# A conditioning projection moved from TensorE matmuls to products summed by VectorE

## The chip, the cores and the metric

The kernel runs as one program on one core of one Trainium2 chip. The metric is the device time of one execution in microseconds (us); lower is better. Inputs are in HBM, in layouts that the host has packed, and everything is float32.

## The reference, cut to what matters

The program is two blocks of a network over 256 tokens of width 1024. The first block is a gated delta rule and a dilated attention side by side (the "mixers"), merged through two gates, and a feed-forward part that gathers expert rows. The second block is conditioned: each of its four sublayers uses a shift, a scale and a gate computed from one vector `c`:

```python
cond = jax.nn.silu(c)                                        # c: (1, 1024)
for layer in range(DEPTH_2):                                 # two layers
    mod = jnp.einsum('bd,sde->sbe', cond, ada_w[layer]) + ada_b[layer][:, None, :]
    ...
    shift, scale, gate = jnp.split(mod[0], 3, axis=-1)
    h = rms_norm(x, norm_g[layer, 0]) * (1.0 + scale[:, None, :]) + shift[:, None, :]
```

`ada_w` has 2 x 2 x 1024 x 3072 values, 48 MB. The result `mod` is 4 x 3072 numbers, held in the kernel as a tile of 128 partitions x 96 columns: column o holds outputs 128 o to 128 o + 127. It depends on `c` and the weights alone, so it can be computed at any time before the second block.

## The kernel before, in words

The kernel is written with a tile framework. The code names the engine of each instruction; a planner, which works with its own cost estimates, then fixes the order on each engine and on each DMA queue, and on the chip every engine runs its list in that order. The planner takes what is ready and prefers what stands earlier in the program; work far down in the program runs early if its inputs are there.

The conditioning runs beside the mixers (`mixers`, L442 on). It is a Python generator, `gen4 = ada_pe(am, 0, 96, NQ[0])` (L452), that the mixers' code advances by `quad()`: two steps before the first norm, one after each of six convolution pairs (L465 on, the quad after L490), one after each of 20 doubling steps of the triangular inverses (L624 to L640), one after each of four steps of the state scan, six in the projections of the second pair of attention heads, one in each of eight softmax blocks. What is left runs in a burst just before the merge (`for _ in gen4`, after L791).

One step of `ada_pe` (L415 to L419) loads a tile of 128 x 4 x 512 weights (1 MB, two buffers) by SyncE's queue and multiplies it by one column of silu(c): four matmuls, each with a single column as its stationary operand, that write rows 0, 32, 64 and 96 of one PSUM bank. Eight steps sum up 2048 outputs as four rows. After eight steps the rows are copied to SBUF by four ScalarE copies of 1 x 512 (L424) into a buffer that GpSimd has cleared (L422), turned to columns by four TensorE transposes (L426), and copied to `mod` by VectorE (L427). There are 48 weight steps and six such ends.

The mixers' own work is a stream of projections. A 512 KB weight tile (`load`, L131, four buffers) is split into a high part by ScalarE (L141) and a low part by VectorE (L142), two buffers each, and TensorE multiplies both against the normed input: 24 matmuls of 128 x 256 for each tile (L159, L160, L162; L265, L266, L270 where tokens are on the output's partitions). Beside them run the convolutions on VectorE (L485, L487), the inverses (TensorE L627, L632, L637; ScalarE L629; VectorE's predicated copies L633 and L638), the scan (L672 to L690) and the attention softmax (L726 to L748). PSUM is eight banks of 2 KB: four for tag `pa`, three for tag `pb`, one for the conditioning's sums (`psx`).

After the merge the branch projection (L805) and the output projection follow; in the latter `ada_done` (L431) adds the bias to `mod`, transposes it and writes it to HBM.

Of the kernel before, what the change touches and what calls it, by code (L numbers as in the profile page):

```python
# [9 lines left out]
F32 = mybir.dt.float32  # L10
# [4 lines left out]
AF = mybir.ActivationFunctionType  # L15
ALU = mybir.AluOpType
AX = mybir.AxisListType
PSUM = bass.MemoryType.PSUM
DRAM = bass.MemoryType.DRAM

P = 128
T = 256
D = 1024
KC = 8
EPS = 1e-6
NEG = -1e30
CAP = 64
NADA = 24
NQ = (2, 2)
NG = 11  # L30


# [16 lines left out]
def body(tc, A, out, stop=None, start=None):  # L49
    nc = tc.nc  # L50
    pe, dve, act, pool, sp = nc.tensor, nc.vector, nc.scalar, nc.gpsimd, nc.sync
# [6 lines left out]
    def pa(shape, name="pa"):  # L58
        return psa.tile(shape, F32, name=name, tag="pa")

    PB = {}

    def open_pb(n):
        PB["es"] = ExitStack()
        PB["b"] = PB["es"].enter_context(tc.tile_pool(name="psb", bufs=n, space=PSUM))
        PB["x"] = PB["es"].enter_context(tc.tile_pool(name="psx", bufs=4 - n, space=PSUM)) if n < 4 else None

    def pb(shape, name="pb"):
        return PB["b"].tile(shape, F32, name=name, tag="pb")
# [7 lines left out]
    x = open_x()  # L77
# [24 lines left out]
    def col(name, i=0, n=None):  # L102
        o = COLS[name][0] + i
        return cols[:, o:o + (1 if n is None else n)]

    ident, iota = C("ident"), C("iota")
    half = [cf[:, NCONST - 2 + i:NCONST - 1 + i] for i in range(2)]
    ones_r = cst.tile([P, P], F32R, name="ones_r")
# [25 lines left out]
    def split(w, n=1024, lo=None, of=None):  # L134
        if of and type(of[0]) is not type(w):
            wh, wl = [of[0].tile([P, n], F32R, name=of[1] + i, tag=of[1], bufs=2) for i in "hl"]
        elif of:
            wh, wl = of
        else:
            wh, wl = [ST["p"].tile([P, 1024], F32R, name="w" + i, tag="w" + i, bufs=ST["sp"]) for i in "hl"]  # L140
        act.copy(wh[:, :n], w[:, :n])  # L141
        (lo or dve).tensor_sub(wl[:, :n], w[:, :n], wh[:, :n].bitcast(F32))  # L142
        return wh, wl
# [94 lines left out]
    def norm_t(pool_, src, a_cols, b_cols, xh, xl, ready=None, copy=None):  # L238

        ss = sums(pool_, 4, "nss") if ready is None else ready  # L240
        xt = [pool_.tile([P, 4, T], F32, name="nxt", tag=f"nxt{i}", bufs=1) for i in range(2)]
        for n in range(4):
            chunk_t(pool_, src, n, ss if ready is None else None, xt[n // 2][:, n % 2 * 2:n % 2 * 2 + 2],
                    copy)
        rs = rstd(pool_, ss, "nr")
        norm_scale([xt[k // 4][:, k % 4] for k in range(KC)], rs, a_cols, b_cols, xh, xl)
        return rs
# [110 lines left out]
    mod = cst.tile([P, 96], F32, name="mod")  # L358
    mod_d = drm.tile([4, 3 * D], F32, name="mod_d")

    def ada(pool_, o0, o1, nw, hl_tag, eng, after=None):

        cs = pool_.tile([P, 8], F32, name="cs", tag="cs", bufs=1)
        act.activation(cs, col("c", 0, 8), AF.Tanh, scale=0.5)
        dve.tensor_scalar(cs, cs, 0.5, 0.5, op0=ALU.mult, op1=ALU.add)
        dve.tensor_mul(cs, cs, col("c", 0, 8))
        pend = []

        def column_sums(acc):
            hl = split(acc, 512, pool, (pool_, hl_tag))  # L370
            ps = pa([P, 512], "ps_ada")
            for i in range(2):
                pe.matmul(ps, ones_r, hl[i][:, 0:512], start=i == 0, stop=i == 1)
            return ps

        def to_columns(o, ps):
            for j in range(4):
                js = slice(j * P, (j + 1) * P)
                dve.tensor_tensor_reduce(ps[:, js], ps[:, js], ident, 1.0, 0.0, ALU.mult, ALU.add, mod[:, o + j:o + j + 1])

        for o in range(o0, o1, 4):
            acc = pool_.tile([P, 512], F32, name="aacc", tag="aacc", bufs=1)
            for k in range(KC):
                w = pool_.tile([P, 512], F32, name="aw", tag="aw", bufs=nw)
                if after is not None and 2 * (o - o0) + k < nw:
                    pool.tensor_copy(w[:, 0:1], after)
                sp.dma_start(w, A["ada_w"][o * 2 + k])
                if k == 0:
                    eng.tensor_scalar_mul(acc, w, cs[:, 0:1])
                elif eng is pool:  # L390
                    pool.tensor_scalar_mul(w, w, cs[:, k:k + 1])
                    pool.tensor_add(acc, acc, w)
                else:
                    dve.scalar_tensor_tensor(acc, w, cs[:, k:k + 1], acc, op0=ALU.mult, op1=ALU.add)
                if k == 4 and pend:
                    to_columns(*pend.pop())
                if k < KC - 1:
                    yield
            pend.append((o, column_sums(acc)))
            yield  # L400
        if pend:
            to_columns(*pend.pop())

    def ada_pe(pool_, o0, o1, nw):


        cs = pool_.tile([P, 8], F32, name="cs", tag="cs", bufs=1)
        act.activation(cs, col("c", 0, 8), AF.Tanh, scale=0.5)
        dve.tensor_scalar(cs, cs, 0.5, 0.5, op0=ALU.mult, op1=ALU.add)
        dve.tensor_mul(cs, cs, col("c", 0, 8))  # L410
        for o in range(o0, o1, 16):
            n = min(4, (o1 - o) // 4)
            ps = PB["x"].tile([P, 512], F32, name="ps_ada", tag="px")
            for k in range(KC):
                w = pool_.tile([P, 4, 512], F32, name="awp", tag="awp", bufs=nw)  # L415
                sp.dma_start(w, A["ada_w"].rearrange("(s j k) p n -> s k p j n", j=4, k=KC)[o // 16, k])
                for j in range(n):
                    pe.matmul(ps[32 * j:32 * j + 1], cs[:, k:k + 1], w[:, j], start=k == 0, stop=k == KC - 1)
                yield  # L419
            pc = pa([P, 4, P], "pc_ada")  # L420
            r = pool_.tile([P, 4, 512], F32, name="arow", tag="awp", bufs=nw)[:, 0]
            pool.memset(r, 0.0)  # L422
            for j in range(n):
                act.copy(r[32 * j:32 * j + 1], ps[32 * j:32 * j + 1])  # L424
            for c in range(4):
                pe.transpose(pc[:, c], r[:, c * P:(c + 1) * P], ident)  # L426
            dve.tensor_copy(mod[:, o:o + 4 * n].rearrange("p (j c) -> p j c", c=4),  # L427
                            pc[:, :, 0:32 * n:32].rearrange("p c j -> p j c"))
            yield

    def ada_done(pool_):  # L431
# [9 lines left out]

    def mixers():  # L442
        es = ExitStack()
        open_pb(3)
        mx = es.enter_context(tc.tile_pool(name="mx", bufs=1))
        am = es.enter_context(tc.tile_pool(name="am", bufs=1))

        def quad(n=1):
            for _ in range(n):
                next(gen4, None)  # L450

        gen4 = ada_pe(am, 0, 96, NQ[0])  # L452
        cx[0] = mx.tile([P, 4 * P], F32, name="cx")
        def tl(shape, name, tag=None, bufs=1, dt=F32, p_=None):
            return (p_ or mx).tile(shape, dt, name=name, tag=tag or name, bufs=bufs)
# [1 line left out]
        with tc.tile_pool(name="nrm", bufs=1) as np_:  # L457
            xh, xl = None, None
            xh = mx.tile([P, KC, T], F32R, name="xh", tag="xh")
            xl = mx.tile([P, KC, T], F32R, name="xl", tag="xl")  # L460
            ws = [load(A["w_in"][i]) for i in range(2)]
            quad(NQ[1])
            norm_t(np_, x, col("norm_mix", 0, 8), None, xh, xl)

        oah = mx.tile([P, 4, T], F32R, name="oah")  # L465
        oal = mx.tile([P, 4, T], F32R, name="oal")
# [6 lines left out]
        with tc.tile_pool(name="cv", bufs=1) as cv:  # L473
            for c in range(0, 12, 2):
# [3 lines left out]
                ps = pa([P, 2, T])  # L478
                proj_pair(ps, A["w_in"][c:c + 2] if c else [lambda: ws[0], lambda: ws[1]], xh, xl, (pool, pool) if c == 0 else (None, None), c == 0)
                act.copy(cin[:, :, 2:T + 2], ps)  # L480
                acc = cv.tile([P, 2, T], F32, name="cacc", tag="cacc", bufs=2)
                th = cv.tile([P, 2, T], F32, name="cth", tag="cth", bufs=2)
                for j in range(2):
                    w = lambda i: col("conv", (c + j) * 4 + i)
                    dve.tensor_scalar_mul(acc[:, j], cin[:, j, 0:T], w(0))  # L485
                    for i in range(1, 4):
                        dve.scalar_tensor_tensor(acc[:, j], cin[:, j, i:i + T], w(i), acc[:, j],  # L487
                                                 op0=ALU.mult, op1=ALU.add)
# [8 lines left out]
                if c == 0:  # L497
                    ab = tl([P, 2, 16], "ab")
                    ps = proj_small(dq, A["w_ab"], 16, xh, xl, "ab")
# [20 lines left out]
                if c == 4:  # L520
                    ps = pa([P, 80])
# [25 lines left out]
            r = stat_rsqrt(cv, pst.rearrange("p a b -> p (a b)"), 8, 1.0, 4 * EPS, "l2")  # L547
            for c in range(0, 8, 2):
                ps = pa([P, 2, T])
                for j in range(2):  # L550
                    stat_bc(ps[:, j], r, c + j)
                dve.scalar_tensor_tensor(qkv[:, c:c + 2], qkv[:, c:c + 2], (P ** -0.5) if c < 4 else 1.0, ps,
                                         op0=ALU.mult, op1=ALU.mult)
# [4 lines left out]
        for b in range(2):  # L558
            for o, base in ((kt, 4), (vt, 8)):
                ps = pa([P, 4, P])  # L560
# [254 lines left out]
                ada_done(am)  # L815
        es.close()
        PB["es"].close()
        open_pb(4)

# [1086 lines left out]
        if stop == "mix":  # L1908
            return finish()
    if start == "peer":  # L1910
        open_pb(4)
        with tc.tile_pool(name="adp", bufs=1) as adp:
            for _ in ada(adp, 0, NADA, 2, "gc", dve):
                pass
# [5 lines left out]
            ST["es"].close()  # L1920
            return finish()
    if start not in (None, "peer"):
        open_pb(4)
        with tc.tile_pool(name="adp", bufs=1) as adp:
            for _ in ada(adp, 0, 96, 2, "gc", dve):
                pass
            ada_done(adp)
# [101 lines left out]
def _pack(I):  # L2029
    v = {}  # L2030
# [64 lines left out]
        mw[:, :, 2 * n:2 * n + 2] = I[nm].reshape(2, 16, 2, 4, P, 512).transpose(0, 1, 2, 4, 3, 5).reshape(2, 16, 2, P, 2048)  # L2095
    mw[:, :, 4:6] = I["moe_w2_2"].reshape(2, 16, 4, P, 2, 512).transpose(0, 1, 4, 3, 2, 5).reshape(2, 16, 2, P, 2048)
    v["moe_w"] = mw
    v["ada_w"] = I["ada_w_2"].reshape(4, 8, P, 6, 512).transpose(0, 3, 1, 2, 4).reshape(192, P, 512)
    return v


# [24 lines left out]
```

## Time and profile before

| | us |
|---|---|
| median of 3 runs | 2070.19 (2065.85 to 2072.55) |
| the profiled execution | 2081.53 |
| its span | 2079.7 |

| engine | busy us | share of the span | instructions |
|---|---|---|---|
| TensorE matmul (PE) | 1833.2 | 88% | 9963 |
| TensorE weight load (PEld) | 1191.3 | 57% | 9963 |
| VectorE (DVE) | 1075.7 | 52% | 2616 |
| ScalarE (ACT) | 603.9 | 29% | 1232 |
| GpSimd (POOL) | 449.4 | 22% | 407 |

The span is the time from the first to the last instruction of the profiled execution. Matmuls are pipelined and the profile models their ends, so a busy TensorE is not TensorE at its peak. The granted clock is the share of full speed that TensorE was given. A float32 matmul is recorded as two instructions. Names such as `awp<-in_ada_w` say what is written from what.

### The profile page before, as it was taken

The numbers are of one execution on the slowest core, as the hardware profiler recorded it, in microseconds if no ns is written. First come the engines' busy times: TensorE is split into PE (matmuls) and PEld (weight loads), VectorE is DVE, ScalarE is ACT, GpSimd is POOL, SyncE is SP. The second block draws the span as 40 slices with busy tenths as digits, with TensorE's granted clock in tenths as the row PEclk, the third lists the DMA queues.
The fourth block names the chain that finished last, engine by engine and source line by source line (L and its number), as shares of the span: only waits on it lengthen the run. The fifth ranks groups of instructions, "written<-read, shape, count | busy, mean of one in ns | idle before, by whom it ended". The sixth has DMA issues, their size and how long they took to land. (4 is left out here: it accounts for less than half of the span.)

```text
span 2079.7 us, 27097 instructions
## 1 busy us (share of the span) xinstructions
PE 1833.2 (88%) x9963; PEld 1191.3 (57%) x9963; DVE 1075.7 (52%) x2616; ACT 603.9 (29%) x1232; POOL 449.4 (22%) x407
## 2 busy tenths in 40 slices
PE   7999999989787787877887789988999899979998
PEld 6787897779743332333333369774444599854443
DVE  6545452346857577577575554763222369642222
ACT  4433342335321111121111143642111364421110
POOL 2100000001454444444444311010000154310000
PEclk8999998999989999999999999898999999989999
DMA  9666643755699999999999957136999483469995
GB/s 320 200 228 192 213 150 100 275 168 167 239 426 427 427 427 426 427 410 427 427 421 427 427 179 268 52 136 285 419 419 419 174 292 119 179 243 419 419 420 226
DMA packets 122679, 624.82 MB, mean 300 GB/s; under 512 B 11535, under 2 KB 16495, under 8 KB 65035
## 3 DMA queue, kind: packets, MB, share of 16 engines
q1 hardware_dynamic: 85675, 354.54, 45.8%
q0 software_dynamic: 36864, 268.45, 30.7%
q8 instruction: 83, 1.36, 0.3%
q14 instruction: 57, 0.46, 0.1%
HBM read 621.80 MB, written 1.16 MB: 300 GB/s over the span
## 5 line engine op out<-in xcount | busy, mean ns | idle before, releaser
L986 PE MATMUL acc<-uv,dg 128*128 128x512 f32 x1024 | 498.6, 645 | 123.7 <-ACT dg L984 123.6
L986 PEld LDWEIGHTS acc<-uv,dg 128*128 128x128 f32 x1024 | 205.9, 206 | 414.4 <-issue 242.3
L974 DVE CUSTOM_DVE_ANT_0 uv<-uv,xn 128x1024 f32<-128x1024 f32 x256 | 316.9, 1242 | 205.7 <-DMA uv<-in_puv,ix 198.9
L973 POOL DMA_INDIRECT uv<-in_puv,ix x256 | 287.5, 1123 | 339.6 <-PE acc L986 236.0
L142 DVE TENSOR_TENSOR wl<-w,wh 128x1024 fp32r<-128x1024 f32 x129 | 160.6, 1249 | 166.8 <-ACT wh L141 109.4
L141 ACT CAST wh<-w 128x1024 fp32r<-128x1024 f32 x166 | 173.6, 1049 | 247.7 <-PE pb L160 71.9
L1631 PE MATMUL ph<-mw,xg 128*64 128x512 f32 x1024 | 226.0, 600 | 6.8 <-DVEq L1557 6.8
L1631 PEld LDWEIGHTS ph<-mw,xg 128*64 128x64 f32 x1024 | 76.1, 138 | 153.3 <-issue 152.2
L142 POOL TENSOR_TENSOR wl<-w,wh 128x1024 fp32r<-128x1024 f32 x37 | 89.0, 2408 | 244.3 <-PE pa L270 158.6
L980 ACT ACTIVATE ac<-ac 128x4 f32<-128x4 f32 (+1 forms) x65 | 13.4, 206 | 430.1 <-DVE ac L974 430.1
L159 PE MATMUL pa<-xh,wh 128*128 128x256 f32 x480 | 121.5, 290 | 2.1 <-ACT wh L141 2.1
L160 PE MATMUL pa<-xl,wh 128*128 128x256 f32 x480 | 119.5, 286 | 0.0
L1667 PE MATMUL pa<-mw,hT 128*64 128x512 f32 x512 | 116.9, 595 | 0.0
L1639 DVE TENSOR_TENSOR h<-h,ph 128x256 f32<-128x256 f32 x32 | 12.0, 418 | 200.5 <-PE ph L1631 200.5
L159 PEld LDWEIGHTS pa<-xh,wh 128*128 128x128 f32 x480 | 93.3, 194 | 6.5 <-ACT wh L141 3.6
L160 PEld LDWEIGHTS pa<-xl,wh 128*128 128x128 f32 x480 | 93.2, 194 | 0.0
L984 ACT ACTIVATE dg<-cf,ac 128x128 f32<-128x128 f32 x256 | 82.5, 392 | 22.1 <-DVE ac L981 20.5
L159 PE MATMUL pb<-xh,wh 128*128 128x256 f32 x352 | 88.4, 287 | 0.0
L160 PE MATMUL pb<-xl,wh 128*128 128x256 f32 x352 | 88.2, 286 | 0.0
L162 PE MATMUL pa<-xh,wl 128*128 128x256 f32 x480 | 69.7, 290 | 19.7 <-POOL wl L142 15.8
L162 PEld LDWEIGHTS pa<-xh,wl 128*128 128x128 f32 x480 | 62.9, 195 | 22.1 <-POOL wl L142 16.6
L1667 PEld LDWEIGHTS pa<-mw,hT 128*64 128x64 f32 x512 | 36.7, 137 | 67.1 <-issue 66.2
(617 smaller groups left out, 2991.7 us busy)
## 6 DMA issues: line engine op xcount, KB each, us to landing
mw<-in_moe_w SPq DMA_DIRECT2D x192, 1024.0 KB, 16.6
awp<-in_ada_w SPq DMA_DIRECT2D x48, 1024.0 KB, 5.6
w<-in_w_in SPq DMA_DIRECT2D x68, 512.0 KB, 5.0
w<-in_hg_c SPq DMA_DIRECT2D x22, 512.0 KB, 4.0
w<-in_wq SPq DMA_DIRECT2D x16, 512.0 KB, 3.6
w<-in_nsa_c SPq DMA_DIRECT2D x16, 512.0 KB, 8.3
w<-in_w_br SPq DMA_DIRECT2D x8, 512.0 KB, 4.3
w<-in_w_out SPq DMA_DIRECT2D x8, 512.0 KB, 3.5
```

Of the source, the lines that this page charges most:

```text
L141: act.copy(wh[:, :n], w[:, :n])
L142: (lo or dve).tensor_sub(wl[:, :n], w[:, :n], wh[:, :n].bitcast(F32))
L159: pe.matmul(ps, wh[:, k], xh[:, k], start=k == 0, stop=False)
L160: pe.matmul(ps, wh[:, k], xl[:, k], start=False, stop=False)
L162: pe.matmul(ps, wl[:, k], xh[:, k], start=False, stop=k == nk - 1)
L973: pool.indirect_dma_start(w, None, A["puv"], bass.IndirectOffsetOnAxis(ap=ix[b][:, k:k + 1], axis=0))
L974: dve.tensor_tensor_reduce(w[:, 0:D], w[:, 0:D], xn[:, b], 1.0, 0.0, ALU.mult, ALU.add, h[:, s:s + 1])
L980: act.activation(hs, hs, AF.Gelu_apprx_tanh)
L984: act.mul(dg, ident, hs[:, i:i + 1])
L986: pe.matmul(acc[b][n], dg, w[:, D + 512 * n:D + 512 * n + 512], start=k == 0, stop=k == P - 1)
L1631: pe.matmul(ps[64 * i:64 * i + 64], xg[:, k, CAP * i:CAP * i + CAP], r3(w[4 * c + 2 * (k // 4) + i], 4)[:, k % 4], start=k == 0, stop=k == ...
L1667: pe.matmul(ps[64 * i:64 * i + 64], hT[:, f, 64 * i:64 * i + 64], w2[n][i][:, f], start=f == 0, stop=f == 3)
```

## The change

`ada` and `ada_pe` are replaced by one generator on VectorE. The host packs `ada_w` as 96 tiles of 128 output columns (partitions) x 1024 inputs, 512 KB each. The row silu(c) is brought to all partitions once (`cr`, a broadcast load of 512 KB, then ScalarE and VectorE on 128 x 1024). One step loads one tile (three buffers of 4 KB for each partition) and runs one `tensor_tensor_reduce`: it multiplies the tile by `cr` in place and writes the sum over the 1024 inputs to one column of `mod`. There are no matmuls, no PSUM bank and no end of a group. `quad` advances two steps; the first quad stands behind the norm instead of ahead of it; tag `pb` gets the fourth PSUM bank.

```diff
-    def open_pb(n):
+    def open_pb():
         PB["es"] = ExitStack()
-        PB["b"] = PB["es"].enter_context(tc.tile_pool(name="psb", bufs=n, space=PSUM))
-        PB["x"] = PB["es"].enter_context(tc.tile_pool(name="psx", bufs=4 - n, space=PSUM)) if n < 4 else None
+        PB["b"] = PB["es"].enter_context(tc.tile_pool(name="psb", bufs=4, space=PSUM))
...
-        for o in range(o0, o1, 16):
-            n = min(4, (o1 - o) // 4)
-            ps = PB["x"].tile([P, 512], F32, name="ps_ada", tag="px")
-            for k in range(KC):
-                w = pool_.tile([P, 4, 512], F32, name="awp", tag="awp", bufs=nw)
-                sp.dma_start(w, A["ada_w"].rearrange("(s j k) p n -> s k p j n", j=4, k=KC)[o // 16, k])
-                for j in range(n):
-                    pe.matmul(ps[32 * j:32 * j + 1], cs[:, k:k + 1], w[:, j], start=k == 0, stop=k == KC - 1)
-                yield
...
+    def ada(pool_, nw):
+        cr = pool_.tile([P, D], F32, name="cr", tag="cr", bufs=1)
+        t = pool_.tile([P, D], F32, name="awt", tag="awt", bufs=nw)
+        sp.dma_start(cr, A["c_row"].to_broadcast([P, D]))
+        act.activation(t, cr, AF.Tanh, scale=0.5)
+        dve.tensor_scalar(t, t, 0.5, 0.5, op0=ALU.mult, op1=ALU.add)
+        dve.tensor_mul(cr, cr, t)
+        for o in range(96):
+            w = pool_.tile([P, D], F32, name="awt", tag="awt", bufs=nw)
+            sp.dma_start(w, A["ada_w"][o])
+            dve.tensor_tensor_reduce(w, w, cr, 1.0, 0.0, ALU.mult, ALU.add, mod[:, o:o + 1])
             yield
...
         def quad(n=1):
-            for _ in range(n):
+            for _ in range(2 * n):
                 next(gen4, None)
-        gen4 = ada_pe(am, 0, 96, NQ[0])
+        gen4 = ada(am, 3)
...
-            quad(NQ[1])
             norm_t(np_, x, col("norm_mix", 0, 8), None, xh, xl)
+            quad(2)
...
-    v["ada_w"] = I["ada_w_2"].reshape(4, 8, P, 6, 512).transpose(0, 3, 1, 2, 4).reshape(192, P, 512)
+    v["ada_w"] = I["ada_w_2"].reshape(4, D, 24, P).transpose(0, 2, 3, 1).reshape(96, P, D)
+    v["c_row"] = I["c_2"][0].reshape(1, D)
```

## Rows read from the trace of the kernel before

**Rows 1.** Stages: length, busy us of PE, PEld, DVE, ACT, POOL; clock, DMA share, GB/s.

```profile
0.00:18.00 18.00, 5.80 (x28) 4.06 (x28) 9.04 (x27) 7.81 (x23) 5.83 (x22) 0.87 0.88 318
18.00:97.00 79.00, 79.00 (x575) 63.79 (x575) 53.38 (x112) 39.34 (x64) 8.95 (x18) 0.94 0.73 241
97.00:320.00 223.00, 218.15 (x1744) 187.68 (x1742) 103.81 (x175) 86.98 (x137) 11.54 (x14) 1.00 0.63 197
320.00:376.00 56.00, 56.00 (x282) 40.49 (x281) 14.98 (x44) 9.08 (x23) 0.00 (x0) 0.76 0.31 107
376.00:443.00 67.00, 67.00 (x551) 59.85 (x549) 28.27 (x38) 28.08 (x34) 0.53 (x1) 1.00 0.78 271
```

**Rows 2.** Who waited for whom up to 465 us: total, times, longest.

```profile
DVE wl L142 <- ACT wh L141: 71.5, 38, 4.9
DVE xt L633 <- PE pa L632: 27.6, 13, 5.2
...
PE ps_ada L418 <- DMA awp<-in_ada_w: 11.2, 6, 4.6
```

**Rows 3.** The conditioning's matmuls alone, by stage (PE, PEld, clock, DMA share, GB/s).

```profile
18.00:97.00 79.00, 11.20 (x66) 1.02 (x66) 0.94 0.73 241
97.00:320.00 223.00, 27.98 (x190) 2.77 (x190) 1.00 0.63 197
320.00:376.00 56.00, 7.73 (x40) 0.53 (x40) 0.76 0.31 107
376.00:443.00 67.00, 7.28 (x56) 0.74 (x56) 1.00 0.78 271
```

**Rows 4.** Around one step, in order of time: start, duration, idle before.

```profile
402.35 1.04 PE L418 MATMUL ps_ada<-awp,cs 128*1 128x512 f32 x8
403.32 0.19 PEld L159 LDWEIGHTS pb<-xh,wh 128*128 128x128 f32 x1 [0.86 <-issue]
```

**Rows 5.** Transposes at one group's end, in order of time.

```profile
121.08 0.60 PE L426 MATMUL pc_ada<-cf,arow 128*128 128x128 f32 x4
```

**Rows 6.** From the last gate tile to the merge, in order of time.

```profile
443.65 1.90 PE L418 MATMUL ps_ada<-awp,cs 128*1 128x512 f32 x16
...
445.86 1.46 DVE L791 TENSOR_TENSOR odl<-od,odh 128x512 fp32r<-128x512 f32 x2
...
450.16 1.89 PE L418 MATMUL ps_ada<-awp,cs 128*1 128x512 f32 x8 [4.62 <-DMA awp<-in_ada_w]
452.15 2.34 ACT L424 COPY arow<-ps_ada 1x512 f32<-1x512 f32 x4 [5.55 <-PE ps_ada L418]
...
455.37 0.56 PE L159 MATMUL pa<-odh,wh 128*128 128x256 f32 x1
...
460.57 0.28 PE L159 MATMUL pa<-odh,wh 128*128 128x256 f32 x1
```

**Rows 7.** Groups on VectorE in the expert stage and in the mixers.

```profile
L974 DVE CUSTOM_DVE_ANT_0 uv<-uv,xn 128x1024 f32<-128x1024 f32 x256 | 316.9, 1242 | 205.7 <-DMA uv<-in_puv,ix 198.9 <-PE acc L986 6.7
...
L142 DVE TENSOR_TENSOR wl<-w,wh 128x1024 fp32r<-128x1024 f32 x70 | 85.4, 1225 | 108.3 <-ACT wh L141 71.5 <-ACT zs L629 12.1 <-PE pb L162 11.4
```

**Rows 8.** A doubling step of the inverse, in order of time.

```profile
226.56 0.73 DVE L633 COPY_PREDICATED xt<-cu,pa 128x512 f32<-128x512 uint8 x1 [0.92 <-PE pa L632]
...
229.54 1.05 PE L627 MATMUL pa<-xt,lm 128*128 128x128 f32 x8
```

**Rows 9.** An operation of the merge that ran before the first norm.

```profile
7.63 0.15 DVE L765 TENSOR_SCALAR onh<-cols 128x1 f32<-128x1 f32 x1
```

**Rows 10.** The stretches in which VectorE is fullest, columns as in Rows 1.

```profile
20.00:40.00 20.00, 20.00 (x168) 17.24 (x164) 16.05 (x37) 11.32 (x21) 5.30 (x9) 1.00 0.95 325
...
460.00:480.00 20.00, 20.00 (x171) 20.00 (x171) 17.26 (x27) 9.29 (x14) 0.00 (x0) 0.99 0.49 159
```

**Rows 11.** DMA issues up to 465 us: count, size, median us to landing.

```profile
awp<-in_ada_w SPq DMA_DIRECT2D x48, 1024.0 KB, 5.6
w<-in_w_in SPq DMA_DIRECT2D x68, 512.0 KB, 5.0
```

More of the change, by code (lines that the diff above doesn't have):

```diff
@@ L27 @@
 CAP = 64
-NADA = 24
-NQ = (2, 2)
 NG = 11
@@ L359, in body @@
     mod_d = drm.tile([4, 3 * D], F32, name="mod_d")
[L361 to L382, printed above, removed]
-            for k in range(KC):
[L384 to L397, printed above, removed]
-                    yield
[L399 to L410, printed above, removed]
-        for o in range(o0, o1, 16):
-            n = min(4, (o1 - o) // 4)
-            ps = PB["x"].tile([P, 512], F32, name="ps_ada", tag="px")
-            for k in range(KC):
-                w = pool_.tile([P, 4, 512], F32, name="awp", tag="awp", bufs=nw)
-                sp.dma_start(w, A["ada_w"].rearrange("(s j k) p n -> s k p j n", j=4, k=KC)[o // 16, k])
-                for j in range(n):
-                    pe.matmul(ps[32 * j:32 * j + 1], cs[:, k:k + 1], w[:, j], start=k == 0, stop=k == KC - 1)
[L419 to L428, printed above, removed]
@@ L443, in mixers @@
         es = ExitStack()
-        open_pb(3)
+        open_pb()
         mx = es.enter_context(tc.tile_pool(name="mx", bufs=1))
@@ L817, in mixers @@
         PB["es"].close()
-        open_pb(4)
+        open_pb()
     def peer():
@@ L1910, in body @@
     if start == "peer":
-        open_pb(4)
+        open_pb()
         with tc.tile_pool(name="adp", bufs=1) as adp:
@@ L1922, in body @@
     if start not in (None, "peer"):
-        open_pb(4)
+        open_pb()
         with tc.tile_pool(name="adp", bufs=1) as adp:
```

## The prediction

> **What bounds the kernel now.** I read the busy times of the whole span first, but they average over unlike parts, so next the stages of the mixers, where the change works [rows 1]. From 18 to 443 us TensorE is busy for 420 of 425 us, VectorE for 200. Then the waits up to 465 us [rows 2]: VectorE's largest is for ScalarE's high part of a weight tile, and its predicated copies wait 27.6 us for matmuls, while TensorE's own largest wait for another engine or a load is 11.2 us, at the conditioning's loads. So TensorE sets the pace between 18 and 443 us, and VectorE and ScalarE follow it. Only around 443 to 455 us does TensorE stand still for something else, and that is the conditioning's own end [rows 6]. At 320 to 376 us its clock is low (0.76 of full speed on the mean, between the two levels of 1.2 and 2.4 GHz).
>
> All sums are made against the profiled execution, 2081.53 us, which is 11.3 us above the median of the runs, 2070.19; I take a difference found in the one over to the other as it is.
>
> **What goes from TensorE.** The conditioning's matmuls take 11.2, 28.0, 7.7 and 7.3 us in the four stages from 18 to 443 us [rows 3], 54.2 us together. That this is time on the path is seen around one step: it starts at 402.35, and the next weight load of the projections starts at 403.32, with 0.86 us of idle put down to issue [rows 4], so a step costs the projections 0.97 us. Of six group ends five lie in these stages. Each has four transposes, 0.60 us on TensorE [rows 5], so 3.0 us more.
>
> **The end of the conditioning.** From 443.65 us TensorE does two steps, waits 4.6 us for a 1 MB load, does another at the low clock (1.89 us), waits for four ScalarE copies (2.34 us) and transposes; the merge's first matmul starts at 455.37 [rows 6]. What it needs of the mixers, `odl`, is ready at 445.86 + 1.46 = 447.32. So 8.0 us go. Its first 5.2 us (455.37 to 460.57, 24 matmuls, 0.22 us each) run at the low clock. At the pace of the projections, (67.0 - 7.3) / (551 - 56) = 0.12 us for each matmul from 376 to 443 us [rows 1, 3], it would be 2.9 us; but TensorE still pauses from 443.65 to 447.3, so I count none of these 2.3 us and keep them for the range.
>
> The most that can go is therefore 54.2 + 3.0 + 8.0 + 2.3 = 67.5 us. ScalarE's 24 copies and GpSimd's clears go too; neither engine is full, so I count nothing for them (ScalarE's copies at a group's end hold up the high parts behind them by 2.3 us; this is inside the give-back below).
>
> **What comes to VectorE.** 96 products of 128 x 1024 with a row sum. The expert stage runs this very form, operands and sizes: 1242 ns on the mean [rows 7]. So 96 x 1.242 = 119.2 us, plus about 2 us once for `cr` (the product like the 1225 ns subtraction of the same size [rows 7], the rest an estimate below that). VectorE has room as a sum: 200 us busy of 425, 321 after, of 368 if all 57 us go. But it would be 87% full on the mean. Its fullest stretches with TensorE undisturbed are 16.05 of 20 us (80%) and 17.26 of 20 (86%) [rows 10].
>
> What stands behind a product on VectorE: the low part of a weight tile (TensorE needs it for the last third of the tile's matmuls, and four raw and two split buffers lie ahead) and the predicated copies of the inverse. For these the rows show the slack. The copy into `xt` ends at 226.56 + 0.73 = 227.29, and TensorE takes `xt` at 229.54 [rows 8]: 2.25 us. One product in between (1.24) is hidden, two (2.48) are not.
>
> When will the planner place them? It lets ready work run far ahead: a line of the merge, L765, ran at 7.63 us [rows 9]. The steps depend on nothing but their loads. On a full TensorE they were left near their place in the program; VectorE has gaps everywhere, so I expect the products to run ahead of the quads' places, many of them by 320 us. Between 18 and 97 us that is costly: 53.4 us are busy already [rows 1], and the 16 products of the quads written there bring 19.9, so 73.3 + 2 for `cr` against 79.0 - 11.2 = 67.8 us of TensorE: VectorE becomes the longer one. From 97 to 320 us it has 103.8 of its own; 52 products (two for each of the 26 steps that ran there) bring 64.6, to 168.4, against some 223 - 28.0 - 1.8 = 193.
>
> Stage by stage, with what I take and both ends:
> - 0 to 18 us: TensorE mostly waits for the first norm here (5.8 us busy, [rows 1]). `cr` and the first products share VectorE with it; but the conditioning's 2 MB of loads now queue on SyncE behind the first weight tiles. +1.5 us (between -2 and +5).
> - 18 to 97: at best -11.2 - 0.6; VectorE's 75.3 allow -3.7. I take -2 (between -12 and +8).
> - 97 to 320: at best -28.0 - 1.8 = -29.8. With VectorE at 87% I give half back: -15 (between -30 and +10).
> - 320 to 376: -7.7 - 0.6 = -8.3 at best; the scan is a chain through VectorE, and a product in front of one of its links costs up to 1.24. -7 (between -9 and +4).
> - 376 to 443: -7.3 at best, VectorE 42% full. -7 (between -8 and 0).
> - 443 to 461: -8.0 (between -10.3 and -3, if the last loads come late for the bias in `ada_done`).
>
> Sum: +1.5 - 2 - 15 - 7 - 7 - 8 = -37.5 us. From 2081.5 that is 2044; as a median of runs 2070.2 - 37.5 = 2032.7, **2033 us**. Everything after the merge is untouched and moves up as it is. The fourth `pb` bank can only take waits off TensorE; I see none of size in [rows 2] and count nothing.
>
> The Trainium skill, "DMA: Bandwidth & Descriptors", section "Rules for kernel authors", asks for 128 partitions and at least 1 MiB in a transfer; the change halves each transfer to 512 KB. The trace agrees so far as 512 KB weight tiles take 5.0 us to landing and 1 MB tiles 5.6 [rows 11], 105 against 187 KB for each us. By that rule alone the loads would pace the products; this is the second rival.
>
> **The rivals.**
> 1. *VectorE becomes the bound (slower).* If the products fill VectorE up to 320 us, it has 53.4 + 103.8 + 121 = 278 us of work there, against 302 - 39.2 - 2.4 = 260 of TensorE. It can't run without gaps, since it also waits for ScalarE and TensorE. At the 80% of the fuller stretch in the convolutions [rows 10] it takes 348 us, 46 more than the 302 of now; the later stages give back 7 + 7 + 8 = 22, so +24, 2094. The point from which it decides: 278 / (302 + 22) = 86% - if VectorE can't hold that beside the chain, the kernel is slower. For it: the convolution stage, and two products in a row exceed the 2.25 us of [rows 8]. Against it: at 86% in 460 to 480 us TensorE did not stall [rows 10], and the planner may spread the products up to 443 us. With gaps the clock could also stay low, as in 320 to 376 us.
> 2. *The loads pace the products (no change).* Three buffers make a round of 5.0 to land [rows 11], 1.24 for the product and some 0.4 to issue (an estimate): 6.6 us for three, 2.2 each, 212 for all. If the planner puts products into VectorE's list sooner than that, each waits at its load and holds what is behind. 0.4 us each, all passed on, is 38 us: the whole gain, 2070. For it: 95% DMA share in 20 to 40 us [rows 10]. Against it: up to 320 us there is room for 136 such products.
> 3. *TensorE's time goes nearly whole.* -62 us, 2008. For it: TensorE never waited for VectorE for long. Against it: VectorE's 87%.
> 4. That the change doesn't do what it says: the matmuls and their bank are gone for certain; only the gain can fail. No chance of its own.
>
> **How the numbers follow.** My forecast, 2018 to 2052, gets 0.42; rival 3 0.18; rival 2, 2064 to 2076, 0.11; rival 1 0.29. For 8 in 10 the range goes from 2004 to 2090. A measurement of this kernel tells some 0.3% (6.2 us) from no change: faster by more than that 0.62 (the first two and a part of the third), within 0.09, slower 0.29.
>
> **What would show it.** Right: no `ps_ada` rows, 96 products of 1.24 us on VectorE; the merge's first matmul about 38 us earlier, within 3 us of `odl`; TensorE still without idle from 97 to 320. Wrong: TensorE waiting for `wl` or `xt` from VectorE by more than some 25 us in total up to the merge; VectorE waiting for the conditioning's loads; a clock below 1.00 in 97 to 320 us; products longer than 1.24.

## The result and the profile after

The changed kernel takes 2098.3 us (median of 4 runs, 2096.39 to 2104.19) against 2071.37 for the kernel before on the same chip: 1.0132 times the time, interval 1.0101 to 1.0163. It is slower, by 27 us, and lies outside the predicted range, which ended at 2090. Its profiled execution takes 2104.19 us, with a span of 2102.4.

From the page of the changed kernel, the busy time of each engine, the group of the products (as in [rows 7]) and the loads (as in [rows 11]):

```profile
PE 1805.5 (86%) x9555; PEld 1212.5 (58%) x9555; DVE 1183.1 (56%) x2802; ACT 591.8 (28%) x1208; POOL 447.1 (21%) x401
...
L370 DVE CUSTOM_DVE_ANT_0 awt<-awt,cr 128x1024 f32<-128x1024 f32 x96 | 118.1, 1235 | 28.1 <-DMA awt<-in_ada_w 27.7
...
awt<-in_ada_w SPq DMA_DIRECT2D x96, 512.0 KB, 5.1
```

The products are as many and as long as foreseen: 118.1 us against 119.2, loads landing after 5.1 us. Where they ran is seen in the operations on their tile (duration in ns as least, median and most; first and last start in us):

```profile
L370 DVE CUSTOM_DVE_ANT_0 awt<-awt,cr x96: 1207/1222/2074, 23.3 to 254.8; 128x1024 f32<-128x1024 f32 x96
```

All 96 lie before 255 us. The quads to which the code ties them reach to the merge; the planner did not wait for these places. The stages, as in [rows 1], and below them the stretch that holds the products:

```profile
0.00:18.00 18.00, 3.65 (x16) 3.28 (x16) 9.93 (x28) 8.82 (x24) 5.84 (x22) 1.00 0.89 306
18.00:97.00 79.00, 70.94 (x481) 65.33 (x482) 74.58 (x142) 33.17 (x52) 7.95 (x14) 0.89 0.87 307
97.00:320.00 223.00, 178.12 (x1299) 171.04 (x1299) 165.71 (x291) 71.32 (x107) 9.81 (x11) 0.87 0.73 240
320.00:376.00 56.00, 50.55 (x376) 47.98 (x375) 30.45 (x69) 19.55 (x37) 1.01 (x3) 0.97 0.18 51
376.00:443.00 67.00, 67.00 (x394) 59.55 (x393) 18.83 (x32) 15.38 (x25) 0.00 (x0) 0.80 0.18 62
18.00:260.00 242.00, 189.06 (x1266) 176.37 (x1267) 212.21 (x398) 78.39 (x123) 16.00 (x23) 0.84 0.86 290
```

Read the last line first. VectorE is busy for 212.2 of 242 us, 88%, and 118 of these are products; TensorE is busy for 189.1, and its granted clock has fallen to 0.84. After 260 us there are no products, and VectorE is hardly fuller than in the kernel before (77.4 against 71.9 us from 260 to 443). The roles have changed only in the first 260 us.

TensorE's waits up to the merge, as in [rows 2], say what it waited for:

```profile
PE pa L324 <- DVE sty L190: 13.5, 1, 13.5
PE pa L569 <- DVE xt L575: 8.6, 3, 3.6
PE rb L223 <- DVE rs_y L190: 7.7, 1, 7.7
...
PE pa L467 <- DVE g L458: 6.3, 1, 6.3
PE pb L681 <- DVE s__2554 L677: 5.9, 1, 5.9
...
PE pb L159 <- DVE wl L139: 4.4, 3, 2.8
PE pa L553 <- DVE dec L550: 2.8, 1, 2.8
PE pa L569 <- DVE xt L564: 2.4, 1, 2.4
```

Nearly all are for VectorE, 57 us with the four shorter ones (2.8 us in the kernel before). No single link carries them: a norm's root, a decay, a softmax step, the inverse. The longest shows the mechanism. It is the root of the q/k norm, a chain of small VectorE operations that ends in `sty`. In the kernel before (start, duration):

```profile
71.68 0.17 DVE L186 TENSOR_SCALAR rs_s<-stv 128x16 uint32<-128x16 uint32 x1
...
72.55 0.17 DVE L187 TENSOR_SCALAR rs_y<-rs_s 128x16 uint32<-128x16 uint32 x1
...
80.49 0.26 DVE L193 SCALAR_TENSOR_TENSOR sty<-rs_f,rs_y 128x16 f32<-128x16 f32 x2
```

and in the changed kernel:

```profile
101.45 0.18 DVE L183 TENSOR_SCALAR rs_s<-stv 128x16 uint32<-128x16 uint32 x1
...
106.34 0.17 DVE L184 TENSOR_SCALAR rs_y<-rs_s 128x16 uint32<-128x16 uint32 x1
106.42 1.22 DVE L370 CUSTOM_DVE_ANT_0 awt<-awt,cr 128x1024 f32<-128x1024 f32 x1
...
118.27 1.23 DVE L370 CUSTOM_DVE_ANT_0 awt<-awt,cr 128x1024 f32<-128x1024 f32 x1 [0.97 <-DMA awt<-in_ada_w]
...
123.22 0.26 DVE L190 SCALAR_TENSOR_TENSOR sty<-rs_f,rs_y 128x16 f32<-128x16 f32 x2
123.53 0.64 PE L324 MATMUL pa<-cf,sty 128*64 128x128 f32 x2 [13.47 <-DVE sty L190]
```

Operations of 0.17 us now stand in one list with products, splits and convolutions that are each ready; the chain takes 21.8 us instead of 8.8, starts 30 us later, and TensorE stands still for 13.5 us at its end.

What all this adds up to is read from one window in each kernel, from the start to the merge's first matmul. Before:

```profile
0.00:455.37 455.37, 431.12 (x3202) 357.57 (x3203) 213.19 (x401) 175.53 (x286) 27.38 (x56) 0.95 0.63 209
```

After:

```profile
0.00:472.59 472.59, 398.65 (x2794) 375.23 (x2795) 315.76 (x586) 162.40 (x261) 24.61 (x50) 0.89 0.60 201
```

TensorE's conditioning was 63.9 us of the 431.1 (59.7 for steps, 4.2 for transposes), so 367.2 us of other work were left. The same work takes 398.7, 31.5 more, at a mean clock of 0.89; and TensorE is idle for 73.9 us instead of 24.3, 49.7 more. -63.9 + 31.5 + 49.7 = +17.3, the 17.2 us by which the merge starts later. The merge then starts as foreseen right at its inputs (as the end of [rows 6]):

```profile
472.59 0.50 PE L156 MATMUL pa<-odh,wh 128*128 128x256 f32 x2 [1.20 <-ACT odh L732]
...
473.54 1.46 DVE L733 TENSOR_TENSOR odl<-od,odh 128x512 fp32r<-128x512 f32 x2
...
474.28 0.39 PE L157 MATMUL pa<-odl,wh 128*128 128x256 f32 x1 [1.18 <-DVE odl L733]
```

This sum is that of two single executions. They are 22.7 us apart, the medians 27. The 5.5 us beyond the 17.2 lie behind the merge, 3.7 of them between the last `acc` matmul of the expert stage and the first `ph` matmul, a stretch that takes between 214.5 and 220.0 us in the runs shown here. And the execution of the kernel before has a clock of 0.76 from 320 to 376 us [rows 1], where that of the burst experiment below, whose source differs only in the gates behind this stage, has 0.97 and does 370 matmuls in place of 282. By these two counts it costs some 13 us, an estimate; this execution lies 11.3 us above its median.

### The profile page after: what moved, and what is told of

The parts are those of the page before. It is cut to its first block, busy times and chain, and to the rows that moved or that the text cites. A ratio compares the mean times of both kernels' runs of the same rounds, so it can differ in the third digit from the quotient of the medians.

```text
span 2102.4 us, 26542 instructions
## 1 busy us (share of the span) xinstructions
PE 1805.5 (86%) x9555; PEld 1212.5 (58%) x9555; DVE 1183.1 (56%) x2802; ACT 591.8 (28%) x1208; POOL 447.1 (21%) x401
## 5 line engine op out<-in xcount | busy, mean ns | idle before, releaser
L370 DVE CUSTOM_DVE_ANT_0 awt<-awt,cr 128x1024 f32<-128x1024 f32 x96 | 118.1, 1235 | 28.1 <-DMA awt<-in_ada_w 27.7
L157 PEld LDWEIGHTS pa<-xl,wh 128*128 128x128 f32 x480 | 94.4, 197 | 0.0
L156 PE MATMUL pb<-xh,wh 128*128 128x256 f32 x352 | 92.8, 297 | 0.7 <-ACT qk L647 0.7
L157 PE MATMUL pb<-xl,wh 128*128 128x256 f32 x352 | 93.1, 297 | 0.0
```

What stands on the lines that cost most here:

```text
L156: pe.matmul(ps, wh[:, k], xh[:, k], start=k == 0, stop=False)
L157: pe.matmul(ps, wh[:, k], xl[:, k], start=False, stop=False)
L370: dve.tensor_tensor_reduce(w, w, cr, 1.0, 0.0, ALU.mult, ALU.add, mod[:, o:o + 1])
```

## The experiments

Each was run beside the kernel before on the same chip, and ratios are to that. Unless said otherwise the edit is to the changed kernel.

**Two buffers.** Fewer tiles may run ahead.

```diff
-        gen4 = ada(am, 3)
+        gen4 = ada(am, 2)
```

> One size changed: two buffers for the conditioning's weight tiles instead of three. Theory A (the planner lets the products run ahead, they fill VectorE from 18 to 260 us and stand between the links of its dependent chains, and TensorE waits): a round is 5.1 us to land, 1.24 for the product and some 0.4 to issue, now for two tiles, so 3.4 us each and about 325 us for 96 instead of 240; VectorE is less full, and the time falls to 2070 to 2088 us. Theory B (the loads: their traffic and their landing hold VectorE and the weight tiles): each product still waits for its load, with less in flight; 2095 to 2110.

2099.57 us, ratio 1.0147 (1.0128 to 1.0166): no gain, and in Theory B's range. The products spread to 323 us and VectorE is less full (193.5 of 242 us up to 260), but it now waits for loads (27.7 us in 22 waits before this edit):

```profile
DVE awt L370 <- DMA awt<-in_ada_w: 54.6, 43, 5.8
```

Fewer products in the early stages alone don't bring the time back. That a product that waits for its load holds up all that stands behind it, and so eats the gain, is my reading; the run doesn't show it by itself.

**Loads held at the quads' places.** GpSimd copies one column of a result of the mixers into the tile ahead of its load, so no load starts before the mixers have reached the place of its quad.

```diff
+            if gate[0] is not None:
+                pool.tensor_copy(w[:, 0:1], gate[0])
             sp.dma_start(w, A["ada_w"][o])
...
-                quad()
+                quad(1, qkv[:, c, 0:1])
```

> Each conditioning load is held until a result of the mixers at its quad's place in the program exists (GpSimd copies one column of it into the tile ahead of the load), so that the products can't run ahead; they and their loads stay as many and as large. Theory A: the saving on TensorE comes through as forecast from the kernel before, 2030 to 2050 us. Theory B: as many loads that land as late, each with VectorE waiting; 2070 or more.

2131.09 us, 1.0295 (1.0278 to 1.0312): much slower. Spreading the products over the mixers was the remedy that I had in mind, and as made here it failed. VectorE's waits are of the same kind and a little longer:

```profile
DVE awt L374 <- DMA awt<-in_ada_w: 59.8, 47, 5.6
```

These waits alone don't explain the loss: they are 5 us longer than with two buffers, and the run is 31 us slower. What makes up the rest stays open.

**No loads.** One tile is loaded once; all products read it and write elsewhere.

```diff
+        w = pool_.tile([P, D], F32, name="awt", tag="awt", bufs=nw)
+        sp.dma_start(w, A["ada_w"][0])
         for o in range(96):
-            w = pool_.tile([P, D], F32, name="awt", tag="awt", bufs=nw)
-            sp.dma_start(w, A["ada_w"][o])
-            dve.tensor_tensor_reduce(w, w, cr, 1.0, 0.0, ALU.mult, ALU.add, mod[:, o:o + 1])
+            y = pool_.tile([P, D], F32, name="awy", tag="awt", bufs=nw)
+            dve.tensor_tensor_reduce(y, w, cr, 1.0, 0.0, ALU.mult, ALU.add, mod[:, o:o + 1])
```

> Leaves out 95 of the 96 weight loads: all products read one tile and write a scratch tile, so mod is not the reference's. Theory A: the products are always ready and run ahead even faster; VectorE is as full, TensorE waits as long: 2090 to 2125 us. Theory B: without the traffic and the landing the loss goes: 2030 to 2070.

2087.27 us, 1.0091 (1.0074 to 1.0108). Without any load the kernel is still slower than before: 11 of the 27 us go by the medians, 8 by the ratios, between the ranges of the two theories. That isn't the price of the loads alone, for the products now run even earlier (the last starts at 211.9 us instead of 254.8). In these two stretches VectorE is full and TensorE far from it:

```profile
40.00:80.00 40.00, 30.00 (x169) 25.94 (x168) 40.00 (x81) 16.25 (x26) 0.41 (x6) 0.74 0.27 91
120.00:160.00 40.00, 17.42 (x126) 16.68 (x127) 39.91 (x70) 7.78 (x13) 9.67 (x7) 0.65 0.16 40
```

**Small products.** All loads, but only 64 of 1024 inputs are multiplied.

```diff
-            dve.tensor_tensor_reduce(w, w, cr, 1.0, 0.0, ALU.mult, ALU.add, mod[:, o:o + 1])
+            dve.tensor_tensor_reduce(w[:, 0:64], w[:, 0:64], cr[:, 0:64], 1.0, 0.0, ALU.mult, ALU.add, mod[:, o:o + 1])
```

> All 96 loads stay, but each product takes only the first 64 of 1024 inputs (some 0.2 us instead of 1.24), so mod is not the reference's. Theory A: VectorE is as free as before and TensorE has lost the matmuls: 2005 to 2030 us. Theory B: the loads run as fast or faster and hold things as much: 2085 to 2105.

2030.51 us, 0.9816 (0.9800 to 0.9833). The products' group on its page:

```profile
L370 DVE CUSTOM_DVE_ANT_0 awt<-awt,cr 128x64 f32<-128x64 f32 x96 | 23.7, 250 | 34.7 <-DMA awt<-in_ada_w 34.5
```

The stretch to 260 us and the window up to the merge, which starts here at 397.9 us:

```profile
18.00:260.00 242.00, 231.80 (x1832) 223.07 (x1833) 157.89 (x446) 104.99 (x163) 16.91 (x26) 0.99 0.92 326
...
0.00:398.00 398.00, 368.23 (x2795) 349.59 (x2795) 227.30 (x586) 160.33 (x261) 23.13 (x50) 0.97 0.69 239
```

This run settles most of the question. The instructions up to the merge and the loads are as many as in the changed kernel; 94.4 us of VectorE's time are gone (118.1 - 23.7). The order is not the same: the planner reckons with the shorter products, and 23 of them start ahead of `sty` where 40 did. So the run takes away VectorE's time and the order that the planner makes of it, both at once. TensorE's 2795 instructions up to the merge now take 368.2 us, close to the 367.2 worked out above, the clock is 0.97, and the idle time is 29.8 us. And DMA is busier (0.92 up to 260 us) with VectorE's waits for loads longer (34.5 us) than in the changed kernel; there they cost little that shows, since VectorE has room to catch up. So TensorE's saving is real, and what eats it is the products' time on VectorE, with the order that comes of it.

**Products held by a gate.** Loads run ahead; the product itself must wait for GpSimd to subtract and add the mixers' column in the tile.

```diff
+            if gate[0] is not None:
+                pool.tensor_sub(w[:, 0:1], w[:, 0:1], gate[0])
+                pool.tensor_add(w[:, 0:1], w[:, 0:1], gate[0])
             dve.tensor_tensor_reduce(w, w, cr, 1.0, 0.0, ALU.mult, ALU.add, mod[:, o:o + 1])
...
-                quad()
+                quad(1, qkv[:, c, 0:1])
```

> As the paced kernel, but the loads are free to run three tiles ahead and only the product is held: GpSimd subtracts and adds a result of the mixers at the quad's place in one column of the landed tile. So VectorE should hardly wait for a load any more (59.8 us in 47 waits in the paced one). Theory C (in the paced kernel the loss was VectorE's list standing at loads): most of it goes, 2035 to 2065 us. Theory D (what counts is VectorE's time itself, 1.24 us in front of a link of a chain that TensorE waits for, wherever the products stand): still 2080 or more.

2140.06 us, 1.0321 (1.0299 to 1.0342). Not a clean run: the wait for loads (59.8 us in the run above) became one for the gate, and a longer one:

```profile
DVE awt L375 <- POOL awt L374: 80.3, 46, 5.4
```

It tells nothing of late products as such, only that on an engine that works through its list in order a held instruction holds all the others.

**Product on GpSimd, sum on ScalarE.** Nothing of it on VectorE.

```diff
-            dve.tensor_tensor_reduce(w, w, cr, 1.0, 0.0, ALU.mult, ALU.add, mod[:, o:o + 1])
+            pool.tensor_mul(w, w, cr)
+            act.activation(w, w, AF.Copy, accum_out=mod[:, o:o + 1])
```

> The changed kernel with the same loads, but GpSimd multiplies (some 2.4 us for 128x1024 by its subtractions of that size) and ScalarE sums (some 1.05 us plus 0.19 for reading the sum): nothing of it on VectorE or TensorE. Theory D (VectorE's time in the chains): 2020 to 2050 us if ScalarE, 40% busy, takes it better. If 1.24 us on any engine of the chains costs the same: 2080 to 2110. Theory B (the loads): 2085 to 2105.

2102.09 us, 1.0141 (1.0120 to 1.0161): as slow as the change, though VectorE has no product. The low part of a weight tile, 1225 ns in [rows 7], takes longer beside GpSimd's products:

```profile
L139 DVE TENSOR_TENSOR wl<-w,wh 128x1024 fp32r<-128x1024 f32 x69 | 114.3, 1659 | 65.7 <-ACT wh L138 58.1 <-POOL awt L370 3.0 <-PE pb L159 2.7
```

So VectorE's work grew anyway. ScalarE's list, too, stood for GpSimd's products, 64.6 us in 49 waits. The run can't show whether ScalarE would carry the sums for nothing.

**The burst alone.** The kernel before, with a `quad()` after each gate tile, so that no steps are left for the burst.

```diff
                     tgs.append(tg)
+                    quad()
```

> The kernel before, on TensorE, with one quad more after each of the eight gate tiles, so that the burst ahead of the merge is gone. Tests the term of 8.0 us for the end of the conditioning: 2058 to 2064 us if it was right; within 0.3% of before if TensorE would have waited there for other work.

2061.74 us against 2073.15, 0.9945 (0.9925 to 0.9965): 11.4 us faster. TensorE is never idle around the merge, at full clock, where the merge was held up for 8 us before [rows 6]. Below are the stage from 320 us on, the window up to the merge's first matmul, and the stretch behind it:

```profile
320.00:376.00 56.00, 56.00 (x370) 41.90 (x369) 18.13 (x48) 14.64 (x30) 0.53 (x1) 0.97 0.43 147
0.00:435.70 435.70, 419.45 (x3203) 349.07 (x3204) 211.87 (x402) 174.38 (x285) 27.31 (x56) 0.99 0.65 216
440.00:480.00 40.00, 40.00 (x340) 40.00 (x339) 28.46 (x43) 17.38 (x23) 0.00 (x0) 1.00 0.56 175
```

In this execution the merge starts 19.7 us earlier than in that of the kernel before; this is more than the run gains, for the reason told above (the clock of 0.76 there). The gain at the conditioning's end needs no VectorE. This kernel, with one line added, beats both.

**Four pieces.** Each product in four of 256 inputs and a sum of the four: the longest instruction shrinks from 1.24 to 0.43 us, the total grows.

```diff
-            dve.tensor_tensor_reduce(w, w, cr, 1.0, 0.0, ALU.mult, ALU.add, mod[:, o:o + 1])
+            part = pool_.tile([P, 4], F32, name="apt", tag="apt", bufs=3)
+            for i in range(4):
+                h = slice(256 * i, 256 * i + 256)
+                dve.tensor_tensor_reduce(w[:, h], w[:, h], cr[:, h], 1.0, 0.0, ALU.mult, ALU.add, part[:, i:i + 1])
+            dve.tensor_reduce(mod[:, o:o + 1], part, axis=AX.X, op=ALU.add)
```

> The changed kernel with each product cut into four of 256 inputs and one small sum over the four: VectorE's time for a tile rises from 1.24 us to some 1.55 (four of 0.34 from start to start by the 128x256 products with a bias in the softmax, and 0.16), but no single instruction stands longer than 0.42 us in front of a link. Theory D1 (what costs is a long instruction ahead of a link): 2055 to 2085 us. Theory D2 (what costs is VectorE's time as a whole, in stages where its lists are full): 30 us more on VectorE, 2105 to 2130.

2115.43 us, 1.0192 (1.0147 to 1.0237): slower than the change by the medians, with intervals that overlap. More of VectorE's time did not make it faster, which fits Theory D2. Theory D1 was not tested: in VectorE's list 354 of the 384 pieces stand four or more in a row, so a link waited for a whole product as before. A window, and the group of the products:

```profile
80.00:120.00 40.00, 28.71 (x235) 28.01 (x233) 39.33 (x151) 13.11 (x15) 0.00 (x0) 0.91 0.90 312
```

```profile
L373 DVE CUSTOM_DVE_ANT_0 awt<-awt,cr 128x256 f32<-128x256 f32 x384 | 145.3, 430 | 14.2 <-DMA awt<-in_ada_w 14.1
```

**Folding on GpSimd.** GpSimd multiplies and adds the halves; VectorE sums 512.

```diff
-            dve.tensor_tensor_reduce(w, w, cr, 1.0, 0.0, ALU.mult, ALU.add, mod[:, o:o + 1])
+            pool.tensor_mul(w, w, cr)
+            pool.tensor_add(w[:, 0:512], w[:, 0:512], w[:, 512:D])
+            dve.tensor_reduce(mod[:, o:o + 1], w[:, 0:512], axis=AX.X, op=ALU.add)
```

> The same loads; GpSimd multiplies (2.4 us) and adds the halves (some 1.2), VectorE only sums 512 columns of the result (some 0.6 us). VectorE gets 58 us instead of 119, GpSimd some 350 of the 440 us there are. Theory D2 (VectorE's time as a whole): the loss against the kernel with short products (2030 us) shrinks in proportion, 2050 to 2075 us. If waits of VectorE for GpSimd's result hold its list instead: 2090 to 2120.

2148.86 us, 1.0377 (1.0336 to 1.0417), the slowest of all and above both ranges. VectorE's own share fell to 64.5 us, but the operations beside GpSimd's took longer, and those with an input in PSUM (the predicated copies) did not:

```profile
L139 DVE TENSOR_TENSOR wl<-w,wh 128x1024 fp32r<-128x1024 f32 x82 | 163.3, 1995 | 27.9 <-ACT wh L138 9.3 <-PE pa L267 8.8 <-PE pb L159 5.3
L372 DVE TENSOR_REDUCE mod<-awt 128x1 f32<-128x512 f32 x96 | 64.5, 678 | 48.9 <-POOL awt L371 48.9
...
L577 DVE COPY_PREDICATED xt<-cu,pa 128x512 f32<-128x512 uint8 x20 | 14.6, 730 | 7.3 <-PE pa L576 7.2
```

GpSimd was the longer engine: its last product starts at 538.3 us, and the merge's first matmul is at 486.2, 30.8 us later than before. About as much again is lost behind that, so this run tells nothing of VectorE's share alone.

**The last third, then the last half, on VectorE.** The kernel of the burst experiment; 64 or 48 of the 96 output columns stay on TensorE and come first, and the rest are products of VectorE, two for each 1 MB load in the same two buffers. What keeps them from running ahead is `cr`: it lies in the pool that the state scan opens (`late["p"]`), and is loaded at 311.0 us in the second run, so the products fall behind the inverses. The edit shown is that for 48.

```diff
...
+            cr = late["p"].tile([P, D], F32, name="cr")
...
+            for o in range(48, 96, 2):
+                w = am.tile([P, 4, 512], F32, name="awp", tag="awp", bufs=NQ[0]).rearrange("p (a b) n -> p a (b n)", a=2)
+                sp.dma_start(w, A["ada_t"][(o - 48) // 2])
+                for j in range(2):
+                    dve.tensor_tensor_reduce(w[:, j], w[:, j], cr, 1.0, 0.0, ALU.mult, ALU.add, mod[:, o + j:o + j + 1])
+                yield
...
+            yield from ada_pe(am, 0, 48, NQ[0])
```

> The kernel before with the gate quads of the earlier run (2061.7 us), but the last 32 of 96 columns are done by VectorE, two products for each 1 MB load, in the scan, the second heads and the gates, where the trace of before shows VectorE 27 to 42% full. 16 TensorE steps (1.1 us) and two group ends (0.6) go, 18.8 us; 40 us come to VectorE. Theory E (a product costs what its stage lacks of VectorE: 0.7 us for each us in the full stages, little in the late ones): 2043 to 2055 us. Theory F (0.7 us for each us anywhere): 2071.

2056.23 us, 0.9938 (0.9916 to 0.9960): just above Theory E's range, far from Theory F's.

> The same with 48 columns on VectorE: 24 TensorE steps and three group ends go (28.2 us), 60 us come, from the scan on. Theory E: 2035 to 2055 us. Theory F: 2075.

2050.12 us, 0.9909 (0.9880 to 0.9938): the fastest kernel of the study and by the ratios 46 us faster than the change, though its interval overlaps that of the burst alone. The products' group, the two late stages, and TensorE's largest wait for VectorE from 300 to 460 us:

```profile
L465 DVE CUSTOM_DVE_ANT_0 awp<-awp,cr 128x1024 f32<-128x1024 f32 x48 | 56.7, 1221 | 3.5 <-DMA awp<-in_ada_t 3.5
```

```profile
320.00:376.00 56.00, 55.50 (x323) 48.73 (x323) 43.60 (x81) 11.91 (x19) 0.00 (x0) 0.82 0.73 262
376.00:443.00 67.00, 64.89 (x519) 64.26 (x517) 61.21 (x100) 29.07 (x39) 0.00 (x0) 0.95 0.86 315
```

```profile
PE pa L701 <- DVE vn L696: 1.4, 2, 1.3
```

VectorE is up to 91% full (61.2 of 67 us) and TensorE is still busy for 64.9. All 96 products made TensorE wait for VectorE 54 us longer in the early stages; half of them make it wait hardly at all in the late ones.

## Why the prediction was wrong

**What was right.** *What goes from TensorE.* 54.2 + 3.0 + 8.0 = 65.2 us were to go. Up to the merge TensorE is 62.9 us less busy in the run with small products (431.1 to 368.2), and by ratios that run gains 38 us with 23.7 us of products still on VectorE. But the term is somewhat too large, since it was read in the execution with the low clock: against the burst run (419.5 us at a clock of 0.99) TensorE is 51.3 us less busy, and 44 steps at the 0.97 us that the prediction itself read for one are 43 us, not 54.2. *The conditioning's end*, -8.0: 11.4 (7.3 to 15.5 by the interval) in the burst experiment, which also counts part of the low clock that I gave nothing for, and the changed kernel starts its merge while `odl` is being made. *The products*: 1235 ns for the predicted 1242. *The first stage*, +1.5: the first norm's matmuls start at 18.15 us instead of 17.20, +1.0. *The run-ahead* was foreseen in direction ("many of them by 320 us"), but it was all of them by 255.

**The step that failed** is "VectorE has room as a sum", and with it the give-back worked out from it: -15 for 97 to 320 us, "half", and -2 for 18 to 97. Over all stages I gave back 65.2 - 37.5 = 27.7 us. The two traces have 81.2: 49.7 of idle TensorE and 31.5 of TensorE's own work, which took longer at a lower clock. Three things were wrong in it.

First, the sum was over the wrong stretch. I spread 121 us over all 368 us up to the merge, 87%, and the planner put 118 of them into 242. By stages I had 16 products up to 97 us and 52 from there to 320; the trace has 29 and 67. Since every product is ready once its load has landed, the stage in which they fall is that in which the list begins, and that is the convolutions, where VectorE had 53.4 of 79 us already [rows 1].

Second, the slack that I looked up was that of one link. I took the two VectorE results that TensorE takes most often, `wl` and `xt`, and named 25 us of waits for these as the sign of failure. They came to 15.4 us (4.4 + 8.6 + 2.4). The other 41 are waits for results that occur once or a few times: `sty`, `rs_y`, `g`, a softmax step. Such a chain has no entry among the waits of before, because VectorE was there in time; it appears only when the engine's list fills up.

Third, I priced TensorE's idle time at itself. With the gaps the granted clock fell to 0.84 on the mean of 18 to 260 us (0.98 in the kernel before), and the same 2795 instructions up to the merge took 398.7 us against 368.2 in the run with small products, where the clock was 0.97. So about 30 us are the clock's, nearly two fifths of what was lost. I had named "a clock below 1.00" as a sign, but put no price on it. Idle time is not the whole of it: from 376 to 443 us, where the scan runs now, the clock is 0.80 with TensorE busy throughout, and at 320 to 376 us of the kernel before, which rival 1 takes for a stage with gaps, it was 0.76 with TensorE busy for 56 of 56 us [rows 1]. What lowered it there no run shows.

**The rivals.** It was rival 1, VectorE as the bound, to which I gave 0.29, and its 2094 is near the measured 2098. But its point of decision was not what decided: VectorE did hold more than 86%, at 88%, and the kernel is slower all the same, since the work was pressed into a shorter stretch and what stood on TensorE's path came late within it. The nearness of the number is partly luck. Rival 2 has a part: VectorE waits for loads 22 times, 27.7 us, and without any loads the kernel gains 8 to 11 us. The rule of the Trainium skill on transfers ("DMA: Bandwidth & Descriptors", "Rules for kernel authors") asks for larger transfers; here it can point at no more than a lesser cost, for with the same 512 KB loads and little work on VectorE the kernel is 38 us faster than before. No run changes the size of a transfer alone. Rival 3 would have come near with no work on VectorE: by the line through the changed kernel (+27.3 us by its ratio, 118.1 us of products) and the small products (-38.1, 23.7), 65.4 / 94.4 = 0.69 us of time for each us of VectorE, none would give about -54 us, an estimate.

**Which part is shown, and which is open.** Shown: the products' time on VectorE in the early stages, with the order that the planner makes of it, is the main cause (small products, and what is left of the loss with no loads), and the loads are not its main part. Whether VectorE's time or the order weighs more no run tells, nor whether shorter instructions would help if they stood singly. Shown too: holding the products back by their loads or a gate is no cure as made here; that the waits in VectorE's list are the reason is argued. For late products the runs give a lower price, if roughly: half of the columns takes 24 steps of 0.97 us [rows 4] and three ends of 0.60 [rows 5] from TensorE, 25 us, and gains 7 against the burst alone by the ratios, so 18 us come back for 57 of products, 0.3 for each; with the two intervals combined 0.2 to 0.45, below the early 0.69. That the stage sets the price is so far supported, but these products also could not run ahead, and no run tells the two apart. Open also is whether products spread evenly without any wait would cost less, and whether ScalarE could take the sums.

## What to carry to other kernels

Under a planner like this one, work that depends on nothing is run as early as its loads allow, so weigh it against the fullness of the stage where the list begins, not of the span or of the place where the code has it; if it is to run late, let something it really uses (a buffer, an earlier phase of the same job) come late. An engine with 15% of room is not free for an engine that waits for many of its short chains: list all results that it hands over in that stage, those without a wait today too. And take the cheap part of a change by itself first: one line in the kernel before brought 11 us, and the whole change lost 27. Last, compare medians before reading a sum of stages off two single executions: here one stage's clock made some 13 us of difference in the same work.

## What the runs showed of the hardware

Several of VectorE's operations on tiles in SBUF take longer while GpSimd runs products and additions there. The subtraction of 128 x 1024, 1225 ns on the mean in the kernel before, took 1659 with GpSimd's products beside it and 1995 with the folding too, in the groups shown above. The convolutions' multiply-add of 128 x 256 (L431 of the folding kernel) went from 498 to 1007, and their first product (one tensor and a column of scalars, L429) from 405 to 990. Predicated copies, which read a matmul's result in PSUM, stayed at 730, and the sums of 512 elements, with one input, had a median of 676 ns and a longest of 689.

These are waits, not a slower run. From the folding run, in order of time:

```profile
30.42 2.38 POOL L370 TENSOR_TENSOR awt<-awt,cr 128x1024 f32<-128x1024 f32 x1
31.64 2.24 DVE L139 TENSOR_TENSOR wl<-w,wh 128x1024 fp32r<-128x1024 f32 x1 [0.45 <-ACT wh L138]
...
43.19 1.21 DVE L139 TENSOR_TENSOR wl<-w,wh 128x1024 fp32r<-128x1024 f32 x1
```

GpSimd's product ends at 32.80 us, and the subtraction that began beside it ends at 33.88, 1.08 us later; the one at 43.19, with GpSimd idle, takes 1.21. Of the 78 subtractions on VectorE up to 545 us, 55 begin while GpSimd runs a product or an addition, and at the median they end 1.08 us after it and take 2.24; the other 23 take 1.21 at the median. So the price of one is what is left of GpSimd's instruction.

The Trainium skill ("GPSIMD Engine Reference", section "1. Specifications") says that the two engines share SBUF interfaces, with contention for VectorE instructions with two SBUF inputs or in a mode that uses two ports. The runs agree for those with two inputs, and add the size; the first product has one tensor as input, and which mode it ran in no trace here shows.
